# Stick-breaking attention by differences of neighbouring values: the scan's running products are the weights, the mask sits in the scan, and GpSimd adds the halves of the heads

## The chip, the cores and the metric

The kernel runs on one core of a Trainium2 chip. The metric is device time in microseconds of the slowest core, here the only one; a kernel's number is the median of its runs. The engines are TensorE (PE in the profile, its weight loads PEld), VectorE (DVE), ScalarE (ACT), GpSimd (POOL) and SyncE (SP), which issues nearly all DMAs here.

## The reference

One encoder layer on 2048 tokens of width 1024, in float32. A normed and modulated input is projected to queries, keys and values of 16 heads of 64. Eight heads do stick-breaking attention, eight do softmax attention within a band of chunks; the outputs are concatenated, projected, and a squared-ReLU MLP follows. The stick-breaking part, for each query block:

```python
z = jnp.einsum('bqhd,bkhd->bhqk', qb, kb).astype(jnp.float32) * scale
strict = s_idx < t_idx
log_beta = jax.nn.log_sigmoid(z)
log_1m_beta = jnp.where(strict, jax.nn.log_sigmoid(-z), 0.0)
suffix = lax.cumsum(log_1m_beta, axis=3, reverse=True) - log_1m_beta
w = jnp.where(strict, jnp.exp(log_beta + suffix), 0.0)
outs.append(jnp.einsum('bhqk,bkhd->bqhd', w.astype(v.dtype), vb))
```

The weight of a key is its own sigmoid times the product of (1 - sigmoid) over all the keys between it and the query.

## The kernel before

The host hands the sequence over in reverse, so a query attends to later positions and the product over the keys between runs forward. All large products are made of three fp32r matmuls on a high and a low part of each operand (`mm3`); `split` makes the parts with an ACT cast and a subtraction on VectorE or GpSimd. Rows are taken in four blocks of 512 tokens (`TB`), numbered 0 to 3, and blocks of the reversed sequence are worked on from 3 down to 0.

**Projection stage** (to about 421 us). A list of jobs, each one piece of the projection weights for one token block, runs on TensorE. `project` (line 343) does one job in four banks; for the stick-breaking values (piece 4) lines 377 to 391 cast each bank [128 tokens x 512] into high and low parts and store them to the scratch `scr_v`. Three such jobs do blocks 3, 2 and 1; that of block 1, `(1, 4, 1)`, is the last job of all, and runs when the first attention units' operands are already loaded. `behind` and `later` are lists of work put off by a number of ticks, one tick per bank; in this stage ACT, VectorE, GpSimd, TensorE and SyncE are kept in program order.

**Attention** (421 to 1372 us). Units are listed in lines 1043 to 1046: for each query block g from 3 to 0, first the stick-breaking units `SB(h, g, c)` for eight heads h and all key blocks c from g to 3, then the chunked units `CA(h, g)`. A unit has four steps, one for each 128 queries. The loop of line 1115 runs one step after the other; eight steps behind (`LAG`) follow the transposes of the weights and the products with the values. In each step some matmuls of a *filler* (the rest of the projection, then output projections) are dealt out by a credit that depends on the step alone. Scores go into one of four banks (`pz`, tag `z`), which the transposed weights share.

A step of a stick-breaking unit has, in `scores` (line 776), two matmuls into a bank `z` and, in the diagonal unit (c equal to g), a third in bfloat16 that adds -1e30 where a key is not ahead of the query (`identb`, `maskb`). In `soft1` (line 787) ACT makes the sigmoid `b` and then, in place, the sigmoid of the negated scores; VectorE scans that one into running products `p`, started by the last product of the unit before (`carry`); GpSimd puts the start into column 0 of `p` and multiplies `b` by `p` shifted by one. The products `b` are the weights; TensorE transposes them (`transposes`), ACT and VectorE split them (`parts`: `wth`, `wtl`), TensorE multiplies them with the parts of the values (`values`) into `acc`, whose two halves of 64 partitions hold the products with the high and the low part.

At the end of a head `finish` (line 693) adds the halves: ACT copies one into `otmp`, VectorE adds the other into `o`. After two heads `keep` (line 705) splits `o` and stores it for the output projection.

The values of block 0 are projected by the filler during attention (`fill_qkv`, line 926); `keep` in line 963 stores them as parts.

## Time and profile before

| | |
|---|---|
| median of 3 runs | 2667.61 us (2666.88 to 2668.83) |
| profiled execution, first to last instruction (span) | 2672.1 us |
| PE busy, matmuls | 2598.4 us (97%) |
| DVE busy | 1929.1 us (72%) |
| ACT busy | 1511.7 us (57%) |
| POOL busy | 919.8 us (34%) |
| attention | 421 to 1372 us of the span |

Of the profiled execution only the span is known. In the rows, tiles are named without their numbers: `z` is a bank of stick-breaking scores, `cz` one of chunked scores, `wt` one of transposed weights, `pt` one of the projection stage, `pf` and `po` those of the filler, `cols` are small columns of the softmax. All the engines' instructions go through one helper (line 42), so the line tells nothing and the tile does. A matmul's end is modelled, so matmuls overlap in the timeline and the time that one takes is read from start to start.

### The profile page before, as it was taken

What the parts mean: (1) busy time and instruction counts of PE and PEld (TensorE: products, weight loads), DVE (VectorE), ACT (ScalarE), POOL (GpSimd) and SP (SyncE); (2) the same over time, 40 slices, a digit from 0 to 9 for tenths busy, and PEclk for the clock granted to TensorE, in tenths of its full rate; (3) what the DMA queues carried; (4) which work ended last, traced back from release to release, by engine and by line L of the source; (5) the groups of instructions that cost most, each with busy time, mean ns of one, the idle gap of its engine ahead of it and who ended that gap; (6) DMA issues with size and microseconds to landing.
All of it is one profiled execution on the core that took longest, in us unless ns stands there. A gap on an engine that the chain in (4) does not pass through costs nothing. (4 is left out here: it accounts for less than half of the span.)

```text
span 2672.1 us, 40291 instructions
## 1 busy us (share of the span) xinstructions
PE 2598.4 (97%) x12944; PEld 2162.5 (81%) x12944; DVE 1929.1 (72%) x3287; ACT 1511.7 (57%) x2962; POOL 919.8 (34%) x1192
## 2 busy tenths in 40 slices
PE   6999999898999999999999999999999999999999
PEld 5888887687878887778788888878888888888887
DVE  7656766698789878989768787677857656555555
ACT  5333436787688878878654444456544545444443
POOL 4330144576467656767522323100002323200000
PEclk9999999999999999999999999999999999999999
DMA  9879888988887687756677777786675343465574
GB/s 339 307 300 363 313 318 261 262 255 258 251 260 249 203 260 251 236 191 206 208 276 274 273 255 266 252 322 221 222 265 175 138 166 140 148 250 197 194 266 156
DMA packets 263061, 651.28 MB, mean 244 GB/s; under 512 B 29632, under 2 KB 61376, under 8 KB 252992
## 3 DMA queue, kind: packets, MB, share of 16 engines
q1 hardware_dynamic: 261552, 643.98, 70.5%
q10 hardware_dynamic: 1296, 4.72, 0.4%
q8 instruction: 103, 1.69, 0.3%
q14 instruction: 110, 0.90, 0.1%
HBM read 457.21 MB, written 191.37 MB: 243 GB/s over the span
## 5 line engine op out<-in xcount | busy, mean ns | idle before, releaser
L42 PE MATMUL ps<-oph,opv 128*128 128x512 f32 x2688 | 612.5, 390 | 0.3
L42 PE MATMUL ps<-h,opw 128*128 128x512 f32 x2664 | 607.0, 390 | 4.3 <-DVE cx L42 4.3
L42 PEld LDWEIGHTS ps<-oph,opv 128*128 128x128 f32 x2688 | 503.8, 188 | 107.0 <-DVE opv L42 1.2
L42 PEld LDWEIGHTS ps<-h,opw 128*128 128x128 f32 x2664 | 500.6, 188 | 110.3 <-DVE cx L42 5.8
L42 POOL TENSOR_TENSOR b<-b,p 128x512 f32<-128x512 f32 (+1 forms) x320 | 360.3, 1126 | 197.9 <-DVE p L42 176.6
L42 DVE TENSOR_TENSOR wtl<-wt,wth 128x512 fp32r<-128x512 f32 (+3 forms) x544 | 290.5, 545 | 52.5 <-ACT wth L42 50.0
L42 ACT CAST wth<-wt 128x512 fp32r<-128x512 f32 (+3 forms) x544 | 257.8, 485 | 118.8 <-PE wt L42 104.0
L42 DVE TENSOR_TENSOR oph<-hw,oph 128x512 fp32r<-128x512 f32 x224 | 156.4, 698 | 220.4 <-ACT oph L42 220.4
L42 ACT CAST oph<-hw 128x512 fp32r<-128x512 f32 x224 | 139.5, 623 | 283.3 <-PE ps L42 267.2
L42 PE MATMUL pt<-w,ht 128*128 128x512 f32 x1248 | 288.7, 391 | 2.2 <-DVE qh L42 2.2
L42 POOL TENSOR_TENSOR ts<-w 128x512 f32<-128x512 f32 x32 | 44.8, 1400 | 668.4 <-DMA w<-in_w_dram 576.7
L42 PEld LDWEIGHTS pt<-w,ht 128*128 128x128 f32 x1248 | 232.8, 188 | 50.5 <-ACT csq L42 2.9
L42 DVE TENSOR_TENSOR_SCAN p<-z,p,zero 128x512 f32<-128x512 f32 x192 | 246.1, 1282 | 34.6 <-ACT z L42 29.2
L42 PE MATMUL acc<-wth,v 128*128 128x512 f32 (+3 forms) x544 | 222.6, 413 | 0.8 <-ACT wth L42 0.8
L42 ACT ACTIVATE b<-z 128x512 f32<-128x512 f32 (+1 forms) x320 | 171.7, 537 | 65.7 <-PE z L42 48.3
L42 PE MATMUL z<-k,q 128*128 128x512 f32 (+3 forms) x640 | 186.5, 373 | 9.7 <-DVE p L42 7.2
L42 POOL TENSOR_TENSOR e<-e,cols 128x640 f32<-128x640 f32 (+4 forms) x128 | 143.2, 1123 | 146.1 <-DVE cols L42 81.3
L42 PE MATMUL acc<-wtl,v 128*128 128x512 f32 (+3 forms) x544 | 187.1, 350 | 0.0
L42 DVE TENSOR_TENSOR opw<-w,opw 128x512 fp32r<-128x512 f32 x127 | 103.8, 819 | 113.1 <-ACT opw L42 113.0
L42 PE MATMUL wt<-ident,b 128*128 128x128 f32 x1088 | 173.3, 275 | 6.8 <-DVE cols L42 5.1
L42 ACT ACTIVATE z<-z 128x512 f32<-128x512 f32 (+1 forms) x320 | 170.4, 532 | 0.0
L42 PEld LDWEIGHTS wt<-ident,b 128*128 128x128 f32 x1088 | 134.8, 142 | 37.9 <-DVE cols L42 6.7
(193 smaller groups left out, 4257.6 us busy)
## 6 DMA issues: line engine op xcount, KB each, us to landing
hw<-scr_hid SPq DMA_DIRECT2D x112, 512.0 KB, 3.9
k<-scr_k SPq DMA_DIRECT2D x272, 128.0 KB, 4.2
v<-scr_v SPq DMA_DIRECT2D x136, 256.0 KB, 4.3
q<-scr_q SPq DMA_DIRECT2D x128, 256.0 KB, 5.4
w<-in_w_dram SPq DMA_DIRECT2D x64, 512.0 KB, 5.2
hw<-scr_s SPq DMA_DIRECT2D x64, 512.0 KB, 4.6
fw<-scr_w SPq DMA_DIRECT2D x28, 1024.0 KB, 7.0
wa<-in_w_ada_dram SPq DMA_DIRECT2D x48, 512.0 KB, 6.3
```

Of the source, the lines that this page charges most:

```text
L42: return lambda *x, **y: self.tc.keep_in_program_order(f(*x, **y))
```

## The change

Let p(t) be the running product up to and with key t. The weight of key t is p(t-1) - p(t), so the output is the first value plus the sum over t of p(t) times (value of t+1 minus value of t), with a zero behind the last value. The change uses that:

- The scan's products are transposed as they are. The first sigmoid, the seed column and GpSimd's product are gone; `p` now lives in the pool of twelve (`zw`) in which `b` lived, and the pool `zp` has four tiles instead of six.
- Stored as values are differences of neighbouring rows. The raw values go to a new scratch `scr_r` (with a row of zeros behind the last), are read back shifted by one row, GpSimd subtracts, and then the difference is split and stored as before.
- The mask is in the diagonal scan: its second operation is the maximum with a tile `held` that is 1 where the key is not ahead of the query and 0 elsewhere, so the product stays 1 up to the query. The mask matmul is gone. The first value of each query tile is gathered into `vcol` by a DMA of single elements and added to the head's output.
- `finish` copies both halves with ACT into `o` and `otmp`; once for two heads, GpSimd adds them and, in a further operation, `vcol`.

```diff
@@ values of blocks 3 to 1, in project and behind it
+                if kind == 2 and not ca:
+                    step_values(tb, tt, ps, nm)
+                    yield
+                    continue
...
+        def step_values(tb, tt, ps, nm):
+            raw = stp.tile([P, TB], F32, tag="qh", name=f"vr{nm}_{tt}", bufs=6)
+            act.copy(raw, ps)
+            sp.dma_start(raw_rows(tb, tt, 1, slice(None))[:, 0], raw)
+            waiting.append((tt, raw))
+            for n in range(1 if tt < 3 else 2):
+                if waiting[0][0] == tt and tt < 3:
+                    break
+                t, r = waiting.pop(0)
+                behind.add(2 + n, lambda t=t, r=r: follow(tb, t, r, nm))
+            if tt == 3:
+                behind.add(2, lambda: first_values(tb, range(NH // 2)))
...
+        def follow(tb, t, raw, nm):
+            nx = stp.tile([P, TB], F32, tag="qh", name=f"vn{nm}_{t}", bufs=6)
+            sp.dma_start(nx, next_rows(tb, t, 1, slice(None))[:, 0])
+            def less():
+                pool.tensor_tensor(nx, nx, raw, op=ALU.subtract)
+            def parts():
...
+                    split(sv[:, :, t % 2, 0, :], sv[:, :, t % 2, 1, :], half)
...
+            behind.add(1, less)
+            behind.add(2, parts)
@@ finish
-            tmp = op.tile([P, TB], F32, tag="otmp", name=f"otmp{u.nm}")
             act.copy(tmp[r : r + HD, :], u.acc[q : q + HD, :])
-            dve.tensor_tensor(o[r : r + HD, :], u.acc[r : r + HD, :], tmp[r : r + HD, :], op=ALU.add)
+            act.copy(o[r : r + HD, :], u.acc[r : r + HD, :])
             if u.h % 2:
-                soon.append(lambda: keep(u, o))
+                soon.append(lambda: total(u, o, tmp))
+        def total(u, o, tmp):
+            pool.tensor_tensor(o, o, tmp, op=ALU.add)
+            if not u.ca:
+                c = vcol[:, u.h // 2, 4 * u.g : 4 * u.g + 4].unsqueeze(2).to_broadcast([P, 4, P])
+                o4 = o.rearrange("p (t c) -> p t c", c=P)
+                pool.tensor_tensor(o4, o4, c, op=ALU.add)
+            soon.append(lambda: keep(u, o))
@@ scores
-                pe.matmul(z[:, :n], self.q[:, 1, qs], self.k[:, c0:], start=False, stop=not self.diag)
-                if self.diag:
-                    pe.matmul(z[:, :P], identb, maskb, start=False, stop=True)
+                pe.matmul(z[:, :n], self.q[:, 1, qs], self.k[:, c0:], start=False, stop=True)
@@ soft1
-                act.activation(b[:, :n], z[:, :n], AF.Sigmoid, scale=0.125)
                 act.activation(z[:, :n], z[:, :n], AF.Sigmoid, scale=-0.125)
-                before = ones[:, 0:1] if self.diag else self.carry[qi]
-                pool.tensor_copy(pt[:, 0:1], before)
...
-                pool.tensor_tensor(b[:, :n], b[:, :n], pt[:, :n], op=ALU.mult)
+                if self.diag:
+                    dve.tensor_tensor_scan(pt[:, :n], z[:, :n], held[:, :n], 1.0, op0=ALU.mult, op1=ALU.max)
+                else:
+                    dve.tensor_tensor_scan(
+                        pt[:, :n], z[:, :n], zero.to_broadcast([P, n]), self.carry[qi], op0=ALU.mult, op1=ALU.add
+                    )
+                self.carry[qi] = pt[:, n - 1 : n]
+                self.ws.append((pt, c0))
@@ start of attention, behind the last job and the first scores
+        behind.flush()
         later.flush()
```

The values of block 0 go the same way through `late_values` and `late_follow`, with `later` for `behind`, in two copies and two differences for each half of the heads.

The order of the instructions where attention begins, first ACT before. Names: `pt_4_1_3` is the last bank of the last values job, `sv` its parts, `px` and `st` are chunked keys; `z_0_3_3_0` is head 0, query block 3, key block 3, step 0.

```order
L42 CAST sv_4_1_2_1_3887<-pt_4_1_2_3861 128x4x64
L42 ACTIVATE st_8_0_2_3897<-px_8_0_2_3892,gqk_s 128x512
L42 ACTIVATE st_8_0_3_3906<-px_8_0_3_3901,gqk_s 128x512
L42 CAST sv_4_1_2_0_3886<-pt_4_1_3_3910 128x4x64
L42 CAST sv_4_1_2_1_3887<-pt_4_1_3_3910 128x4x64
L42 ACTIVATE b_0_3_3_0_3977<-z_0_3_3_0_3941 128x512
L42 ACTIVATE z_0_3_3_0_3941<-z_0_3_3_0_3941 128x512
```

ACT after, at the same place; `vr` are raw values, `vn` the shifted ones, which by then hold the differences.

```order
L42 ACTIVATE st_8_0_3_3957<-px_8_0_3_3952,gqk_s 128x512
L42 COPY vr_4_1_3_3986<-pt_4_1_3_3961 128x512
L42 CAST sv_4_1_0_0_3995<-vn_4_1_0_3941 128x4x64
L42 CAST sv_4_1_0_1_3996<-vn_4_1_0_3941 128x4x64
L42 CAST sv_4_1_0_0_3995<-vn_4_1_1_3989 128x4x64
L42 CAST sv_4_1_0_1_3996<-vn_4_1_1_3989 128x4x64
L42 CAST sv_4_1_2_0_4017<-vn_4_1_2_4001 128x4x64
L42 CAST sv_4_1_2_1_4018<-vn_4_1_2_4001 128x4x64
L42 CAST sv_4_1_2_0_4017<-vn_4_1_3_4003 128x4x64
L42 CAST sv_4_1_2_1_4018<-vn_4_1_3_4003 128x4x64
L42 ACTIVATE z_0_3_3_0_3992<-z_0_3_3_0_3992 128x512
```

Before, two casts straight from the bank stand between the last bank and the first sigmoid; now a copy and the casts of all four differences do. VectorE's eight subtractions stand ahead of its first scan in the same way.

TensorE at this place, before; `k` and `q` are the operands of the scores.

```order
L42 MATMUL pt_4_1_3_3910<-w_4_7_3728,ht_7_2636 128x512 x3
L42 MATMUL z_0_3_3_0_3941<-k_0_3_3_3768,q_0_3_3765 128x512 x2
L42 LDWEIGHTS identb
L42 MATMUL z_0_3_3_0_3941<-maskb,identb 128x128
L42 MATMUL z_0_3_3_1_3984<-k_0_3_3_3768,q_0_3_3765 128x384 x2
```

TensorE after; `pf` is the filler.

```order
L42 MATMUL pt_4_1_3_3961<-w_4_7_3781,ht_7_2689 128x512 x3
L42 MATMUL z_0_3_3_0_3992<-k_0_3_3_3826,q_0_3_3823 128x512 x2
L42 MATMUL z_0_3_3_1_4065<-k_0_3_3_3826,q_0_3_3823 128x384 x2
L42 MATMUL z_0_3_3_2_4075<-k_0_3_3_3826,q_0_3_3823 128x256 x2
L42 MATMUL z_0_3_3_3_4083<-k_0_3_3_3826,q_0_3_3823 128x128 x2
L42 MATMUL z_1_3_3_0_4089<-k_1_3_3_3832,q_1_3_3829 128x512 x2
L42 MATMUL pf_2_0_4092<-ht_0_2682,fw_2_0_4068 128x512 x3
```

The mask's weight load and matmul are gone from each diagonal step; the first filler matmul stands behind the fifth scores, as before.

More of the change, by code (lines that the diff above doesn't have):

```diff
@@ L115, in encoder_kernel @@
     make_identity(nc, ident)
-    identb = cpool.tile([P, P], BF16, name="identb")
-    dve.tensor_copy(identb, ident)
-    maskb = cpool.tile([P, P], BF16, name="maskb")
-    pool.memset(maskb, 0.0)
-    pool.affine_select(
-        out=maskb, in_=maskb, pattern=[[1, P]], base=0, channel_multiplier=-1,
-        compare_op=ALU.is_gt, fill=NEG,
-    )
+    vcol = cpool.tile([P, 2, NH // 2, 4 * NTB], F32, name="vcol")[:, 0]
+    pool.memset(vcol, 0.0)
     ones = cpool.tile([P, P], F32, name="ones")
@@ L664, in encoder_kernel @@
         sp = nc.sync
+        held = kp0.tile([P, TB], F32, tag="held", name="held", bufs=1)
+        pool.memset(held, 0.0)
+        pool.affine_select(
+            out=held[:, :P], in_=held[:, :P], pattern=[[1, P]], base=0, channel_multiplier=-1,
+            compare_op=ALU.is_gt, fill=1.0,
+        )
         def load_q(ca, h, g):
@@ L972, in fill_qkv, with late_values, late_follow, less @@
                     yield keep
+        raws = {}
+        def late_values(tb, hf, j, ps, nm):
+            cols = slice(hf * CW, (hf + 1) * CW)
+            raw = raws[j] = fp.tile([P, 2, CW], F32, tag="vr", name=f"vr{nm}", bufs=2)
+            act.copy(raw, ps.rearrange("p (t c) -> p t c", t=2))
+            sp.dma_start(raw_rows(tb, 2 * j, 2, cols), raw)
+            if not j:
+                return
+            for i in range(2):
+                later.add(1 + i, lambda i=i, raw=raws[i]: late_follow(tb, hf, i, raw, nm))
+            later.add(2, lambda: first_values(tb, (2 * hf, 2 * hf + 1)))
+        def late_follow(tb, hf, j, raw, nm):
+            nx = xrp.tile([P, 2, CW], F32, tag="xr", name=f"vn{nm}_{j}")
+            sp.dma_start(nx, next_rows(tb, 2 * j, 2, slice(hf * CW, (hf + 1) * CW)))
+            def less():
+                pool.tensor_tensor(nx, nx, raw, op=ALU.subtract)
+            def parts():
+                store_v(0, nx.rearrange("p t c -> p (t c)"), fp, hf, tb, j, f"{nm}_{j}")
+                stepped.add((tb, hf, j))
+            later.add(1, less)
+            later.add(2, parts)
+        stepped = set()
         def outproj(self, g):
```

43 lines of the change are left out of this document (32 added, 11 removed).

## The prediction

> **What bounds the kernel now.** I read the stages first: busy time of each engine in the eight stretches of attention (for the query blocks 3, 2, 1, 0 in turn: stick-breaking units, then chunked units). The columns are the stretch, its length, then PE, weight loads, DVE, ACT and POOL busy, the granted clock and the DMA share.
>
> ```profile
> 421.00:470.00 49.00, 46.39 (x268) 36.17 (x267) 38.33 (x64) 38.27 (x99) 32.66 (x61) 0.97 0.92 275
> 470.00:526.00 56.00, 46.09 (x258) 38.21 (x256) 37.43 (x135) 38.74 (x107) 27.15 (x38) 0.91 0.94 269
> 526.00:649.00 123.00, 118.56 (x758) 102.32 (x757) 106.92 (x150) 101.86 (x220) 84.66 (x136) 0.99 0.79 247
> 649.00:737.00 88.00, 80.13 (x463) 67.93 (x462) 62.34 (x220) 56.95 (x130) 42.79 (x35) 0.94 0.88 264
> 737.00:928.00 191.00, 187.66 (x1193) 161.91 (x1193) 170.98 (x226) 158.19 (x328) 130.01 (x197) 1.00 0.75 235
> 928.00:1009.00 81.00, 78.49 (x517) 69.50 (x515) 64.48 (x223) 57.67 (x133) 43.10 (x36) 1.00 0.89 267
> 1009.00:1272.00 263.00, 256.15 (x1408) 209.69 (x1408) 233.72 (x298) 213.00 (x426) 193.94 (x280) 0.99 0.68 218
> 1272.00:1372.00 100.00, 96.02 (x583) 81.57 (x582) 76.22 (x250) 66.54 (x152) 49.50 (x43) 1.00 0.66 206
> sum 951.00, PE 909.50 PEld 767.31 DVE 790.42 ACT 731.21 POOL 603.82; mean PE 113.69 PEld 95.91 DVE 98.80 ACT 91.40 POOL 75.48
> ```
>
> TensorE is busy 909.5 of 951 us: 41.5 us is all the idle time there is to win. The clock column adds a little: 0.03 x 49 + 0.09 x 56 + 0.01 x 123 + 0.06 x 88 + 0.01 x 263 is about 16 us of lost speed. VectorE is nearly as full in the stick-breaking stretches (233.7 of 263), so it is the second bound. After 1372 us the change touches nothing.
>
> Next, who ended the idle time between 421 and 1372: first TensorE's waits, then VectorE's (us in total, times, longest).
>
> ```profile
> PE wt L42 <- DVE cols L42: 9.3, 6, 2.5
> PE z L42 <- DVE p L42: 7.2, 11, 2.3
> PE cz L42 <- DVE cols L42: 6.2, 9, 1.8
> PE pf L42 <- DMA fw<-scr_w: 5.7, 2, 3.8
> PE cz L42 <- DMA k<-scr_k: 5.6, 3, 2.6
> DVE wtl L42 <- ACT wth L42: 50.0, 93, 7.2
> DVE p L42 <- ACT z L42: 46.1, 95, 2.8
> DVE o L42 <- ACT otmp L42: 28.1, 41, 1.4
> ```
>
> TensorE waits 22.7 us for VectorE and 11.3 us for weights and keys. VectorE in turn waits 46.1 us for the sigmoid ahead of its scan and 28.1 us for the copy ahead of a head's sum. No engine waits long for GpSimd's product.
>
> **The change part by part.** The groups of instructions that it removes (count | busy, mean ns | idle before):
>
> ```profile
> L42 ACT ACTIVATE b<-z 128x512 f32<-128x512 f32 x224 | 134.4, 600 | 50.4 <-PE z L42 37.5 <-POOL p L42 7.0 <-POOL b L42 3.0
> L42 POOL TENSOR_TENSOR b<-b,p 128x512 f32<-128x512 f32 x224 | 289.5, 1292 | 179.5 <-DVE p L42 164.7 <-DVE cols L42 9.9 <-DMA k<-scr_k 0.8
> L42 DVE TENSOR_TENSOR o<-acc,otmp 64x512 f32<-64x512 f32 x64 | 44.0, 687 | 28.5 <-ACT otmp L42 28.1
> L42 PE MATMUL z<-maskb,identb 128*128 128x128 bf16 x128 | 29.6, 231 | 0.0
> ```
>
> *Mask matmuls.* 128 of them go, with their weight loads. The 231 ns overlap their neighbours, so the slot has to be read from the timeline: a full-width step with the mask, then one without.
>
> ```profile
> 1240.20 0.62 PE L42 MATMUL z<-k,q 128*128 128x512 f32 x2
> 1240.67 0.23 PE L42 MATMUL z<-maskb,identb 128*128 128x128 bf16 x1
> ...
> 1247.62 0.63 PE L42 MATMUL z<-k,q 128*128 128x512 f32 x2
> 1248.09 0.62 PE L42 MATMUL po<-fx,ow 128*128 128x512 f32 x2
> ```
>
> From scores to what follows the pair is 0.47 us in both; the filler behind the mask began at 1240.71, so the mask takes 0.04 us. 128 x 0.04 = 5 us gained on TensorE itself; 29.6 us is the upper end.
>
> *The first sigmoid, the product and its seed.* 172 us of ACT and 360 us of GpSimd go, mostly hidden. What shows is the 46.1 us in which the scan waited for ACT: the remaining sigmoid now comes first, one activation (0.6 us) sooner.
>
> *A head's sum.* VectorE loses 64 x 0.687 = 44 us and the 28 us of waits before them. ACT gains 64 copies of about 0.58 us into the 172 us it loses; GpSimd gains 32 + 16 sums of about 1.29 us into the 360 us it loses. Their rows:
>
> ```profile
> L42 ACT COPY otmp<-acc 64x512 f32<-64x512 f32 x64 | 37.2, 582 | 2.8 <-PE acc L42 1.3
> L42 POOL TENSOR_TENSOR os<-o,os 128x512 fp32r<-128x512 f32 x32 | 41.1, 1286 | 17.3 <-ACT os L42 16.3
> ```
>
> The block's output is up to 2.6 us later, hidden by the filler; behind the last unit, some 18 us lie between its store and the first product with the reloaded tiles (1373.6 and 1391.8). Without that cover it would cost 2.6 us once.
>
> ```profile
> L42 ACTq DMA_DIRECT2D scr_m<-os x1: 325/325/325, 1373.6 to 1373.6; - x1
> L42 PE MATMUL pso<-opm,ow x72: 389/389/389, 1391.8 to 1407.9; 128*128 128x512 f32 x72
> ```
>
> *What that relief is worth.* VectorE is relieved of some 118 us of work and waiting, but TensorE can only give back what it loses: 22.7 us behind VectorE and about 16 us of clock. The filler's matmuls are dealt out by step, so where TensorE is full nothing moves. I take half of the waits (11), a fifth of the clock (3) and 5 us for idle time shorter than the modelled end of a matmul: 19 us. From below 5 (all hidden), from above 40 (all of the 22.7, the 16 and a bit).
>
> *Neighbour differences in the projection stage.* Blocks 3 and 2 each get four copies, stores, shifted reloads and GpSimd differences in place of casts straight from the bank. The stretch holding most of them:
>
> ```profile
> 200.00:300.00 100.00, 100.00 (x458) 83.13 (x457) 61.90 (x106) 40.37 (x79) 2.40 (x9) 1.00 1.00 370
> ```
>
> TensorE is full, ACT and GpSimd have room; the DMA engines are full. About 4.2 MB more at 370 GB/s is 11 us of transfer time, hidden because TensorE waits for no load there; with that cover gone, up to 11 us. I take 1. The gathers of first values have no row here: between nothing and a key load's landing each, waited for by GpSimd alone; 0. Block 0's values come late, among the filler: four copies and four differences on engines that have room, no scan behind them; 0.
>
> *The start of attention.* This is the cost. The last values job (block 1) finishes as attention begins, and its parts are flushed there: ACT's and VectorE's queues have its eight casts and eight subtractions ahead of the first sigmoid and scan, and they wait for store, reload and difference. TensorE has only four scores to do; the fifth needs a bank that the first scan frees. Queued behind that wait are the filler on TensorE and every soft step on ACT and VectorE. Before (scores, the last cast; loads and stores with KB and median us to landing; the landing line is that of the value stores; an issue on SyncE; a diagonal scan):
>
> ```profile
> 421.14 0.61 PE L42 MATMUL z<-k,q 128*128 128x512 f32 x2
> 424.88 0.98 PE L42 MATMUL z<-k,q 128*128 128x512 f32 x2 [1.22 <-DVE p L42]
> 421.34 0.37 ACT L42 CAST sv<-pt 128x256 fp32r<-128x256 f32 x1 [3.88 <-PE pt L42]
> v<-scr_v SPq DMA_DIRECT2D x136, 256.0 KB, 4.3
> scr_x<-xr SPq DMA_DIRECT2D x21, 256.0 KB, 3.9
> DMA to landing us min/median/max: 2.9/6.5/8.5
> 427.90 0.58 SPq L687 DMA_DIRECT2D v<-scr_v  x1
> L42 DVE TENSOR_TENSOR_SCAN p<-z,zero 128x512 f32<-128x512 f32 x32 | 39.1, 1222 | 14.7 <-ACT z L42 12.5 <-PE z L42 1.2 <-issue 0.7
> ```
>
> After: copy 421.3 to 421.9; store landed 3.9 later (425.8); SyncE issues two loads of 0.58 ahead (1.2), the reload lands 4.3 later (431.3); difference 1.3, two casts 0.75, sigmoid 0.6, scan 1.2: 435.2. The fifth scores move from 424.9 to 435.2, 10.3 us later. With both transfers at 6.5 us it is 15.1; with 2.9 us each, 8. On SyncE four gathers and four stores of parts stand ahead of the fourth unit's operands, and the stores wait for VectorE; that unit scores twelve steps in, so nobody waits. On GpSimd only the mask tile's setting and the differences themselves are queued.
>
> *The clock there.* Two stretches around the present stall:
>
> ```profile
> 421.80:425.20 3.40, 1.66 (x11) 1.20 (x11) 2.40 (x4) 2.99 (x9) 0.23 (x1) 1.00 0.92 337
> 425.20:428.60 3.40, 3.40 (x10) 2.36 (x9) 2.59 (x4) 1.18 (x3) 3.17 (x6) 0.50 1.10 384
> ```
>
> A stretch in which TensorE was half idle is followed by 3.4 us at half clock, 1.7 us of work lost. That loss exists already, and a longer stall should bring at most one more such stretch: 0 to 1.7, I take 1. The Trainium skill (TensorE: Matmul & The Clock Gate, What's actually happening) says that the clock falls to half after at least one idle window of about 3.4 us and returns after one busy window. The trace agrees on length and ratio, but shows it for 1.74 us of idle in 3.4. By the page's rule the long stall pays one gated window, as now, and the sum would have 0 here.
>
> **The sum.** -5 (mask) - 19 (waits, clock) + 10.3 + 1 (start) + 1 (projection) = -11.7 us on a span of 2672.1: 2660.4. The profiled span lies 4.5 us above the median of the runs, 2667.6; carried over, the forecast is 2656.
>
> **The rivals.** *The start costs more than attention gives back.* Place: 421 to 440 us. Two full-price transfers make the stall 15.1, the clock 1.7 and the projection stage 2; attention returns only the mask's 5 and another 4, because the filler paces it. That is +9.8: 2677.4. It decides once the stall costs more than the waits return. For it: the queues' order makes the chain certain, and DMA is at 0.92 or more there. Against it: 22.7 us of TensorE's waits name VectorE, which gets 12% of the 951 us back. Chance 0.17.
>
> *A wash.* The stall at 10.3 and the gains at 11 cancel: 2667. It holds if half-idle VectorE waits are replaced by waits for the filler's weights. Chance 0.14.
>
> *VectorE was the real bound.* Then nearly all of the 22.7 goes, half of the clock's 16, and short idle time doubles to 10: 5 + 22 + 8 + 10 against 12 is -33: 2635. For it: 89% in the longest stretch, and scan plus subtraction fill a step. Against it: the same stretch has TensorE at 97%. Chance 0.17.
>
> *The change does not do what it says.* The maximum in the 128 diagonal scans could be dearer than the addition. The present ones take 1222 ns for 512 columns, 2.4 ns each; 32 rows of 512 + 384 + 256 + 128 columns make 98 us, and at twice the price as much again would land on a full VectorE: some 80 us slower than the forecast.
>
> Against it: nothing but the operation differs; 0.03, outside the range.
>
> **How the numbers follow.** Forecast 0.49 at 2656, larger gain 0.17, wash 0.14, slower 0.17, dear scan 0.03. The forecast's own bounds (gains of 18 to 34, costs of 10 to 14) run from 2644 to 2664. The range takes in the larger gain and most of the slower case: 2634 to 2675. A measurement tells about 0.2% (5.3 us) from no change, so faster means below 2662.3: the larger gain and most of the forecast and a bit of the wash, 0.66. Same 0.15, slower (above 2672.9) 0.19.
>
> **What would show it.** Right: no mask rows; the scan's wait for ACT well below 46.1 us; TensorE idle some 10 us between 423 and 436 with ACT's casts of the differences just before the first sigmoid; TensorE's waits for VectorE near half. Wrong: the stall under 5 or over 16; attention from the first block's fifth scores to the last sum shortened by less than 10 us or more than 35; diagonal scans above 1.3 us; waits for loads in the projection stage.

## The result

| | before | after |
|---|---|---|
| median, same chip | 2668.22 us (2666.88 to 2669.58, 4 runs) | 2689.03 us (2687.63 to 2689.82, 4 runs) |
| ratio, 95% interval | | 1.0076 (1.0061 to 1.0090) |
| span of the profiled execution | 2672.1 us | 2688.0 us |
| first attention scores | 421.1 us | 442.0 us |
| first scores to the output projection (`pso`) | 970.7 us | 968.4 us |

The change is slower, by 0.8%, where it was forecast to be faster, and lies above the predicted range of 2634 to 2675. By the spans +15.9 us: +20.9 before attention begins, -2.3 in attention, -2.7 behind it. (The span of the profiled execution of before lies 3.9 us above the median in this table; the ratio is the better measure of the whole, the spans of where it lies.) Ratios are taken between runs of the same round and leave out single runs far off the rest, such as one of 9155 us among the six of two_late_sbuf.

### The profile after

The stages of attention, in the order and columns in which the prediction shows them for before:

```profile
442.00:500.00 58.00, 43.12 (x234) 36.24 (x233) 37.97 (x66) 32.37 (x78) 11.14 (x9) 0.85 0.89 262
500.00:556.00 56.00, 46.48 (x259) 37.92 (x259) 32.45 (x130) 43.61 (x118) 32.65 (x39) 0.94 0.98 280
556.00:672.00 116.00, 113.81 (x723) 101.22 (x724) 98.17 (x137) 80.88 (x163) 18.10 (x17) 0.99 0.81 257
672.00:761.00 89.00, 77.56 (x459) 65.44 (x459) 58.53 (x215) 58.91 (x135) 46.08 (x37) 0.96 0.88 263
761.00:962.00 201.00, 189.07 (x1167) 166.71 (x1166) 166.52 (x216) 124.77 (x248) 23.55 (x19) 0.97 0.74 233
962.00:1041.00 79.00, 77.51 (x514) 68.95 (x514) 61.63 (x219) 60.46 (x138) 46.16 (x38) 1.00 0.91 274
1041.00:1293.00 252.00, 247.61 (x1378) 206.70 (x1376) 225.27 (x284) 162.97 (x309) 36.95 (x33) 1.00 0.71 228
1293.00:1391.00 98.00, 95.42 (x587) 81.87 (x586) 70.94 (x241) 70.17 (x160) 55.27 (x48) 1.00 0.68 206
```

Two stick-breaking stretches became shorter (123 to 116, 263 to 252), and two longer: the first (49 to 58) and that of query block 1 (191 to 201), where TensorE now idles 12 us. GpSimd is nearly empty (37 us busy of 252 in the longest stretch, 194 of 263 before). So the work is gone, but time was added in these two places, and in a third, ahead of attention.

TensorE's longest waits in attention, and the scan's wait for the sigmoid (us in total, times, longest):

```profile
PE z L42 <- DVE p L42: 27.5, 9, 14.1
PE pf L42 <- DMA fw<-scr_w: 8.1, 1, 8.1
PE wt L42 <- DVE cols L42: 5.7, 5, 1.8
PE cz L42 <- DMA k<-scr_k: 4.4, 3, 2.5
DVE p L42 <- ACT z L42: 57.8, 107, 3.3
```

Scores wait 27.5 us for a bank that a scan frees, 7.2 before, 14.1 of them in one piece. The scan's own wait for ScalarE, which was to fall well below 46.1 us, rose to 57.8.

Groups that the change altered (the remaining sigmoid, the full-width diagonal scan, the heads' sum, the second copy):

```profile
L42 ACT ACTIVATE z<-z 128x512 f32<-128x512 f32 x224 | 130.7, 584 | 48.5 <-PE z L42 45.3 <-DVE p L42 1.2
L42 DVE TENSOR_TENSOR_SCAN p<-z,held 128x512 f32<-128x512 f32 x32 | 39.0, 1218 | 19.8 <-ACT z L42 19.8
L42 POOL TENSOR_TENSOR o<-o,otmp 128x512 f32<-128x512 f32 x32 | 41.4, 1292 | 285.3 <-ACT o L42 244.0 <-DMA q<-scr_q 27.7 <-DMA k<-scr_k 13.4
L42 ACT COPY o<-acc 64x512 f32<-64x512 f32 x64 | 37.2, 581 | 0.8
```

The scan with the maximum takes 1218 ns, 1222 with the addition: that rival is out.

**Ahead of attention.** Rows picked from the timeline of after, from 285 us: SyncE's issues (SPq), ScalarE and GpSimd around the differences (in brackets, how long the engine sat idle before and what ended that), and TensorE's first product for the last block's norm (`pva`).

```profile
288.68 6.16 SPq L42 DMA_DIRECT2D scr_w<-w  x8
291.88 0.41 ACT L42 CAST sv<-vn 128x256 fp32r<-128x256 f32 x1 [13.52 <-DMA scr_v<-sv]
294.88 0.60 SPq L42 DMA_DIRECT2D vn<-scr_r  x1
301.28 1.29 POOL L42 TENSOR_TENSOR vn<-vn,vr 128x512 f32<-128x512 f32 x1 [13.39 <-DMA vn<-scr_r]
302.60 0.72 ACT L42 CAST sv<-vn 128x256 fp32r<-128x256 f32 x2 [7.76 <-POOL vn L42]
303.22 5.01 ACT L42 ACTIVATE ht<-xt,mod 128x512 fp32r<-128x512 f32 x8
305.31 5.31 SPq L42 DMA_DIRECT2D xt<-in_xT_dram  x8
319.65 1.87 PE L42 MATMUL pva<-ones,nsaa 128*128 128x1 f32 x8 [15.41 <-DVE nsaa L42]
```

The same two steps before the change:

```profile
281.50 5.03 ACT L42 ACTIVATE ht<-xt,mod 128x512 fp32r<-128x512 f32 x8
285.80 6.80 SPq L42 DMA_DIRECT2D xt<-in_xT_dram  x8
```

`ht` is block 1's input, cast from the tiles `xt`; block 0's inputs are loaded into the tiles that it frees. ScalarE, in its order, has the casts of block 2's differences ahead of `ht`. It waits 13.5 us for a staging tile whose store is queued on SyncE, then 7.8 us for a difference whose reload SyncE issued at 294.88, behind eight weight stores. So `ht` comes 21.7 us later, the loads of block 0's inputs 19.5 us later, and TensorE, which had waited for no load here, stands for 15.4 us, until the sums over the late inputs (`nsaa`) are made. Behind that it works until about 326 us at a granted clock of 0.50 (1.00 there before), which costs some 3 us more of the 20.9.

**The start of attention.** The timeline of after, TensorE's fifth scores:

```profile
457.44 1.22 PE L42 MATMUL z<-k,q 128*128 128x512 f32 x2 [14.07 <-DVE p L42]
```

Stretches of 3.4 us around it, in the columns of the stages (length, PE, weight loads, DVE, ACT, POOL, clock, DMA share, GB/s):

```profile
442.00:445.40 3.40, 1.37 (x9) 1.15 (x7) 0.76 (x2) 1.20 (x3) 0.00 (x0) 1.00 1.01 282
445.40:448.80 3.40, 0.00 (x0) 0.00 (x0) 0.00 (x0) 0.00 (x0) 0.00 (x0) 0.53 0.96 333
...
455.60:459.00 3.40, 1.55 (x4) 1.27 (x5) 3.40 (x6) 1.65 (x6) 0.00 (x0) 0.50 0.81 287
459.00:462.40 3.40, 3.40 (x10) 2.82 (x9) 1.36 (x2) 0.35 (x2) 0.00 (x0) 0.50 1.00 285
462.40:465.80 3.40, 3.40 (x20) 2.86 (x20) 2.14 (x4) 1.62 (x5) 0.00 (x0) 0.96 0.21 62
```

The stall is the predicted one, 14.1 us long, with no engine busy at all in the second stretch. From the first to the fifth scores it is 15.4 us (442.0 to 457.4), 3.7 before. The clock returns only after one full stretch of work, 459.0 to 462.4. (The Trainium skill, TensorE: Matmul & The Clock Gate, What's actually happening, says that one busy window of about 3.4 us restores it; this trace agrees.)

**Block 0's late values.** The timeline of after, TensorE's scores in block 1's stretch:

```profile
893.83 1.22 PE L42 MATMUL z<-k,q 128*128 128x512 f32 x2 [6.11 <-DVE p L42]
```

The waits from 885 to 896 us:

```profile
ACT svf L42 <- POOL vnf L42: 7.2, 1, 7.2
DVE svf L42 <- ACT svf L42: 7.0, 1, 7.0
PE z L42 <- DVE p L42: 6.1, 1, 6.1
POOL vnf L42 <- DMA vnf<-scr_r: 5.3, 1, 5.3
```

The casts of `vnf`, the late differences, come two ticks behind their reload; every sigmoid and scan behind them waits too. A second such stall, of 3.7 us, follows near 930 us. In this stretch TensorE idles some 10 us more than in the kernel without the differences (below), and is busy 5 to 6 us longer at a clock of 0.97 where that one has 1.00; these make up the 15 us by which the stretch is longer.

### The profile page after: what moved, and what is told of

Its sections match the earlier page's. It is cut to its first block, busy times and chain, and to the rows that moved or that the text cites. A ratio compares the mean times of both kernels' runs of the same rounds, so it can differ in the third digit from the quotient of the medians.

```text
span 2688.0 us, 38753 instructions
## 1 busy us (share of the span) xinstructions
PE 2583.0 (96%) x12816; PEld 2163.1 (80%) x12816; DVE 1884.6 (70%) x3222; ACT 1417.6 (53%) x2722; POOL 604.2 (22%) x617
## 5 line engine op out<-in xcount | busy, mean ns | idle before, releaser
L42 PE MATMUL z<-k,q 128*128 128x512 f32 (+3 forms) x640 | 186.8, 374 | 29.9 <-DVE p L42 27.5
L42 PE MATMUL wt<-ident,p 128*128 128x128 f32 x1088 | 172.2, 274 | 4.4 <-DVE cols L42 2.9
L42 PEld LDWEIGHTS wt<-ident,p 128*128 128x128 f32 x1088 | 134.8, 141 | 35.3 <-DVE cols L42 5.7
L42 PE MATMUL po<-fx,ow 128*128 128x512 f32 x576 | 160.3, 393 | 0.0
L42 PEld LDWEIGHTS z<-k,q 128*128 128x128 f32 x640 | 115.1, 191 | 52.5 <-DVE p L42 31.5
```

The source lines that it names most:

```text
L42: return lambda *x, **y: self.tc.keep_in_program_order(f(*x, **y))
```

## The experiments

The theory after reading the traces is called Q in the expectations: attention gives back about what was forecast, and making the differences costs some 40 us in three places, because ScalarE and VectorE stand, in order, behind casts that wait for a reload. Rival B says that it is not the order but the bytes, which stand on full DMA engines and on SyncE's queue ahead of the loads that matter. Kernels named plain, idle or free, and the one without gathers, leave a part of the computation out, as said for each; all others compute the whole layer.

### The change without its differences: plain_values

This kernel casts the value parts straight from the banks, and leaves out the raw copies, their stores and reloads, the differences and the first values.

```diff
-                if kind == 2 and not ca:
-                    step_values(tb, tt, ps, nm)
...
-                            late_values(tb, hf, j, ps, nm)
+                            store_v(0, ps, fp, hf, tb, j, nm)
...
```

> The changed kernel, but the value tiles are cast straight from their PSUM banks as before: no raw copy, store, shifted reload, difference or gather (the differences and the first values are left out of the computation; the scan, the mask and the heads' sums stay as changed). Theory Q (the attention stage gives back about what the prediction took, and the making of the differences costs about 40 us by itself: 20.9 in the projection stage, 9.2 at the start of attention, 9.5 where block 0's values come late): 2689 - 40 = 2649, first attention scores at 419 to 424 us. Rival W (attention gives back little, the filler paces it, and the cost of the differences is mostly the shift that they put on everything behind): 2665 or more.

2639.43 us (2638.44 to 2641.98), 0.9902 of before (0.9886 to 0.9917). The stretch from first scores to `pso`, before and here:

```profile
421.10:1391.80 970.70, 929.20 (x5521) 783.59 (x5521) 798.22 (x1572) 736.49 (x1597) 605.11 (x823) 0.98 0.77 241
```

```profile
421.50:1359.70 938.20, 902.36 (x5394) 774.72 (x5393) 753.82 (x1506) 635.00 (x1340) 262.42 (x232) 0.99 0.80 248
```

The scan, mask and sums alone gain 32.5 us in the profiled executions, and 26 us (22 to 30) by the ratio; theory Q expected too small a gain (2649), rival W is out. Its first five stretches:

```profile
421.50:464.80 43.30, 40.75 (x234) 34.26 (x233) 35.05 (x60) 29.60 (x71) 7.24 (x6) 1.00 1.01 294
464.80:520.40 55.60, 46.51 (x260) 37.75 (x258) 32.67 (x131) 43.85 (x118) 32.67 (x39) 0.94 1.00 285
520.40:636.20 115.80, 113.77 (x723) 101.15 (x723) 97.90 (x137) 80.72 (x163) 17.99 (x17) 0.99 0.82 255
636.20:725.80 89.60, 78.17 (x465) 66.02 (x464) 59.16 (x216) 59.29 (x136) 46.07 (x37) 0.96 0.88 267
725.80:911.20 185.40, 183.11 (x1162) 161.90 (x1161) 164.53 (x216) 122.63 (x242) 18.52 (x15) 1.00 0.76 241
```

Against this kernel the whole change loses 20.5 us before attention, 14.5 at its start (57.8 against 43.3 us to the first chunked scores) and 15.1 in block 1's stick-breaking stretch (200.5 against 185.4): together 50.1, of 51.3 us between the spans.

### The traffic with nobody waiting: idle_reload, free_reload

idle_reload keeps copies, stores, reloads and gathers, but casts the parts from the banks and leaves the differences out:

```diff
                     step_values(tb, tt, ps, nm)
-                    yield
-                    continue
...
-            behind.add(1, less)
-            behind.add(2, parts)
...
```

> As plain_values, but the raw copies, their stores, the shifted reloads and the gathers are all issued where the changed kernel issues them; only nothing waits for what they bring (the parts are cast from the banks; the differences are left out). Theory Q (the cost is ScalarE waiting in its order behind parts that wait for the reload and for the landing of the value store): within 4 us of plain_values, 2649 to 2653, first scores before 426 us. Rival B (the cost is the traffic and the issue time on SyncE, 4.2 MB more in a stage whose DMA engines are full): 15 us or more above plain_values, first scores at 435 or later.

2665.37 us (2662.33 to 2676.65), ratio 0.9991 (0.9976 to 1.0006); first scores at 436.2. Q's bound, within 4 us of plain_values, is missed (26 us above it); B's is met. Its `ht` casts and its loads:

```profile
282.29 5.02 ACT L42 ACTIVATE ht<-xt,mod 128x512 fp32r<-128x512 f32 x8
...
300.41 6.42 SPq L42 DMA_DIRECT2D xt<-in_xT_dram  x8
```

`ht` is on time, and still block 0's loads are issued 14.6 us later than before: SyncE gets to them late. That is about the worth of 4.2 MB at 370 GB/s, 11.3 us by estimate, and of the gathers, 3.9 us by the run without them (below). The start of attention loses to the traffic alone as well: 52.8 us to the first chunked scores, against 43.3 in plain_values and 57.8 in the change, with 1.4 us of waits for a scan in all, but one of 5.0 us for a load. In block 1's stretch, though, nothing is lost (185.8 us): there it is the waiting, not the traffic.

free_reload is idle_reload with reloads that read the same number of bytes from the input; it asks whether SyncE was late because it waits, in order, for each raw store to land:

```diff
-            sp.dma_start(nx, next_rows(tb, t, 1, slice(None))[:, 0])
+            sp.dma_start(nx, xT[t * P : (t + 1) * P, tb * TB : (tb + 1) * TB])
```

> As idle_reload (which had its first attention scores at 436.2 and 2665 us, against 421.5 and 2639 without the traffic), but the shifted reloads of blocks 3, 2 and 1 read as many bytes, in the same rows of 2 KB, from the input, so that they wait for no store to land (differences left out). Theory B (bytes: 4.2 MB at the 370 GB/s of that stage are 11 us, the gathers 4): no change, first scores 434 to 437, 2661 to 2668. Rival O (SyncE waits in its order for each raw store to land, and all later loads stand behind): first scores at 428 or earlier, 2655 or less.

2665.59 us, ratio 0.9988 (0.9979 to 0.9998), first scores at 435.1. No change: rival O is out.

### Another queue, and no gathers: reload_gp, no_gathers

reload_gp is the whole change with the shifted reloads of blocks 3 to 1 issued by GpSimd:

```diff
-            sp.dma_start(nx, next_rows(tb, t, 1, slice(None))[:, 0])
+            pool.dma_start(nx, next_rows(tb, t, 1, slice(None))[:, 0])
```

> The changed kernel, whole, with one edit: the shifted reloads of blocks 3, 2 and 1 are issued by GpSimd, on its own DMA queue, not by SyncE behind the bulk stores of weights. Theory Q (the reload comes late because it stands behind those stores on SyncE's queue): most of the 20.9 us of the projection stage returns, first scores at 424 to 432, 2689 - 10 to 18 = 2671 to 2679. Rival B (traffic): no change, 2685 to 2692. Rival G (the gathers): no change either. A third possibility: GpSimd, waiting in its own order for the store to land, delays the norms' reciprocal roots, and the gain is halved.

2693.35 us, ratio 1.0106 (1.0089 to 1.0123), first scores at 443.1. Q's number is missed, and the time is next to B's 2685 to 2692: `ht` comes 4 us sooner than in the change (299.2) and the loads still later (307.2). The reloads land no faster from there (median 5.1 us on either queue).

no_gathers leaves the first values at zero:

```diff
-                behind.add(2, lambda: first_values(tb, range(NH // 2)))
...
-            later.add(2, lambda: first_values(tb, (2 * hf, 2 * hf + 1)))
```

> The changed kernel without the twelve gathers of first values (the first values stay zero: that part of the sum is left out). Theory Q: they hold SyncE for 3.4 us ahead of the store that ScalarE waits for, so 3 to 8 us come back in the projection stage, and 2 to 4 where block 0's values come late: 2678 to 2684. Rival G (the 4-byte transfers are what is dear: they crowd the DMA engines): the whole 20 us come back, 2665 to 2670. If they are hidden, as the prediction took: 2686 to 2691.

2686.26 us, ratio 1.0078 (1.0060 to 1.0096); first scores at 438.1, 3.9 us sooner than in the change. The time lies at the edge of what was expected if they are hidden (2686 to 2691), and by the ratio nothing can be told; by the trace of one execution the gathers, taken at 0, are worth 3.9 us ahead of attention. G is out.

### Two terms of the gain: plain_oldsum, plain_maskmm

Both are plain_values with one thing of before put back.

```diff
-            act.copy(o[r : r + HD, :], u.acc[r : r + HD, :])
+            dve.tensor_tensor(o[r : r + HD, :], u.acc[r : r + HD, :], tmp[r : r + HD, :], op=ALU.add)
```

> As plain_values (2639 us), but a head's two halves are added by VectorE from the bank as before the change (64 adds of 0.69 us), and GpSimd adds only the first values. Theory V (VectorE's share is what the attention stage gives back): 8 to 15 us slower than plain_values, 2647 to 2654, the attention stage (first scores to the output projection, 938.2 us in plain_values) 946 to 953. Rival F (the shorter feed of the scan, one sigmoid in place of two, gave it back; the sum was hidden): 0 to 3 us slower.

2643.02 us (2642.48 to 2644.36): 3.6 slower than plain_values, in the profile 943.9 against 938.2 us of attention. Between the two theories: 64 sums of 0.69 us and their waits were worth a tenth to a fifth of what attention gave back.

```diff
-                pe.matmul(z[:, :n], self.q[:, 1, qs], self.k[:, c0:], start=False, stop=True)
+                pe.matmul(z[:, :n], self.q[:, 1, qs], self.k[:, c0:], start=False, stop=not self.diag)
+                if self.diag:
+                    pe.matmul(z[:, :P], identb, maskb, start=False, stop=True)
```

> As plain_values (2639 us), but the 128 mask matmuls of before are put back behind the scores of the diagonal tiles (the scan keeps its mask tile; the result of the scan is the same). The prediction's term: 128 x 0.04 = 5 us slower, 2644. Upper end of the prediction: 29.6 us of busy time, 2669. If TensorE has slack there: 2639 to 2641.

2644.55 us, 5.1 slower, in the profile 6.6 (944.8). The prediction's 128 x 0.04 = 5 us is met; the upper end, 29.6, is far off. The intervals of these two ratios (0.9891 to 0.9920 and 0.9902 to 0.9937) overlap with that of plain_values, so the times alone don't show either cost; the medians and the stretches agree in sign.

### The waits moved: late_wide, start_later, both_late

late_wide puts the steps of block 0's late values further apart, and its gathers four ticks later:

```diff
-                later.add(1 + i, lambda i=i, raw=raws[i]: late_follow(tb, hf, i, raw, nm))
+                later.add(4 + i, lambda i=i, raw=raws[i]: late_follow(tb, hf, i, raw, nm))
...
-            later.add(1, less)
-            later.add(2, parts)
+            later.add(3, less)
+            later.add(5, parts)
```

> The changed kernel, whole, with only the steps between block 0's late values moved: reload 4 and 5 steps after the store (was 1 and 2), difference 3 steps behind the reload (was 1), parts 5 (was 2). Theory Q (ScalarE and VectorE, in order, stand behind parts that wait for store, reload and difference): most of the 15 us that the stretch of stick-breaking for block 1 has over plain_values comes back, 2689 - 11 to 15 = 2674 to 2678, and no stall of TensorE near 888 and 930 us. Rival B (the traffic there): no change, 2685 to 2690.

2680.81 us, ratio 1.0043 (1.0028 to 1.0058), against 1.0076 for the change. Block 1's stretch falls from 200.5 to 186.7 us and the two stalls are gone, as Q said; 8 us of the time, not 11 to 15.

start_later takes block 1's differences out of the start of attention; they come from step 8 on, with the raw rows reloaded too, and with the casts five steps behind the reload:

```diff
+            if tb == 1:
+                return
             waiting.append((tt, raw))
...
+            later.add(8 + 6 * n, lambda hf=hf, j=j: late_follow(1, hf, j, None, f"e1_{hf}"))
```

> The changed kernel, whole, with one thing moved: block 1's values, whose job ends as attention begins, are only copied and stored there; their reload (raw and shifted rows), difference, casts and parts come from step 8 of attention on, in four portions. Theory Q (the stall at the start is the chain store, reload, difference, casts ahead of the first sigmoid): the stretch from the first scores to the first chunked scores falls from 57.8 to 43 to 46 (43.3 with no differences at all), 2689 - 12 to 15 = 2674 to 2677. Rival B (what is late at the start is the backlog of transfers; with nothing waiting for the reload the stretch still took 52.9): 52 to 54, 2684.

2683.80 us, ratio 1.0047 (1.0029 to 1.0065). The stretch falls from 57.8 to 48.9 us: between the two theories. As this edit takes away both the waiting and the transfers at that place, it can't tell the two apart; idle_reload (52.8 us) says that the transfers had a large part. The stall is gone; but TensorE still waits 6.6 us for scans ahead of scores and 3.9 us ahead of chunked ones, where block 1's portions now stand.

both_late has the two edits together.

> start_later and late_wide together, whole. Theory Q, additive: 2689 - 8 - 13 = 2667 to 2669, level with before; the projection stage keeps its 20 us. Rival B: 2675 to 2677.

2670.45 us, ratio 1.0000 (0.9986 to 1.0014). By the stretches the two add up: 49.9 us at the start, 185.3 in block 1's. Of the 28.9 us by which its span still exceeds that of plain_values, 20.3 lie ahead of attention, in the projection stage, and 6.6 at the start.

### Fewer bytes: sbuf_shift, sbuf_112, sbuf_after

sbuf_shift is both_late with blocks 3 and 2 shifted from one SBUF tile to the next, not by way of DRAM, and with all gathers of first values in attention:

```diff
-            sp.dma_start(nx, next_rows(tb, t, 1, slice(None))[:, 0])
+            sp.dma_start(nx[0 : P - 1, :], raw[1:P, :])
+            sp.dma_start(nx[P - 1 : P, :], scr_r[r : r + 1, :] if up is None else up[0:1, :])
```

> both_late, whole, and blocks 3 and 2 are shifted by one row without the way through DRAM: one transfer from rows 1 to 127 of the raw tile to rows 0 to 126 of the next one, and one of a single row; only each tile's first row is stored, and the gathers of first values come in the first steps of attention. Theory B (bytes ahead of the next block's inputs set the delay): 2.1 MB in place of 4.2 and no gathers, 6 us in place of 15 to 20: first scores at 426 to 429, both_late minus 13 to 16. Rival Q2 (ScalarE's wait for the reload, not the bytes): the chain is one transfer shorter, first scores at 430 to 436. If a transfer within SBUF is dearer than one to DRAM and back: no change.

2737.15 us, ratio 1.0238 (1.0219 to 1.0257): half the bytes, and 67 us slower than both_late. Neither B nor Q2 expected that. From 240 to 280 us, and within it two stretches in which hardly anything but the shifts is moved:

```profile
240.00:280.00 40.00, 21.18 (x97) 17.40 (x95) 3.91 (x9) 4.89 (x11) 5.57 (x8) 0.77 0.32 117
...
248.00:250.00 2.00, 2.00 (x11) 1.65 (x10) 0.00 (x0) 0.00 (x0) 0.00 (x0) 1.00 0.07 26
250.00:252.00 2.00, 2.00 (x11) 1.65 (x10) 0.00 (x0) 0.00 (x0) 0.00 (x0) 1.00 0.07 26
```

The DMA engines are busy 0.32 of the time, moving 117 GB/s, and during the shifts 0.07, moving 26 GB/s: that is about one engine in 16 (0.06). SyncE's issues of `vn<-vr` take up to 9.3 us each. sbuf_after, with block 2's shifts put further back, only moves this:

> As sbuf_shift, whole, and block 2's shifts are put six jobs later, behind the loads of the last block's inputs. Theory B: half of the remaining bytes leave the path too, first scores at 421 to 425, 3 to 5 us below sbuf_shift, 2646 to 2652, against 2639 for no differences at all. Rival: ScalarE's casts, now later, delay the next block's normalization instead, and nothing or less is gained.

2729.95 us, ratio 1.0198 (1.0175 to 1.0220). sbuf_112 is sbuf_shift with the 127 rows cut in two:

```diff
-            sp.dma_start(nx[0 : P - 1, :], raw[1:P, :])
+            for lo, hi in ((0, 112), (112, P - 1)):
+                sp.dma_start(nx[lo:hi, :], raw[lo + 1 : hi + 1, :])
```

> sbuf_shift (2737 us) with one edit: the transfer of 127 rows is issued as one of 112 and one of 15 rows. Theory E (127 rows are dealt to one of the 16 DMA engines, 127 x 84 ns = 10.7 us, while 112 are dealt out evenly): first scores at 426 to 435, 2655 to 2665. Rival S (a transfer from one SBUF tile to another is slow by itself, or the small transfers are): 2720 or more, first scores at 490 or later.

2668.60 us, ratio 1.0000 (0.9990 to 1.0009). One edit returns the 67 us; the same window:

```profile
240.00:280.00 40.00, 40.00 (x186) 33.34 (x185) 24.59 (x43) 13.28 (x31) 10.54 (x13) 1.00 0.83 285
```

So theory E holds in its mechanism: the transfer of 127 rows was not spread over the DMA engines. (The Trainium skill, DMA: Bandwidth & Descriptors, Why a DMA increments its semaphore by 16 and not by 1, says that the number of engines is the largest up to 16 that divides the row count, so that 127 rows use one; the share of 0.07 agrees.) But its number is missed: first scores at 437.8, only the gathers' 4 us better than both_late. Halving the bytes by itself bought nothing:

```profile
298.21 5.02 ACT L42 ACTIVATE ht<-xt,mod 128x512 fp32r<-128x512 f32 x8
300.40 7.51 SPq L42 DMA_DIRECT2D xt<-in_xT_dram  x8
```

Here the loads follow `ht` at once, and `ht` is late behind the casts. There are two chains, the loads' place on SyncE's queue and `ht` behind the casts, and the later one decides:

| kernel | `ht` cast from | `xt` loads from | first scores |
|---|---|---|---|
| before | 281.5 | 285.8 | 421.1 |
| plain_values | 281.8 | 286.5 | 421.5 |
| idle_reload (traffic, no order) | 282.3 | 300.4 | 436.2 |
| free_reload | 280.3 | 298.6 | 435.1 |
| no_gathers | 299.4 | 301.5 | 438.1 |
| sbuf_112 (order, less traffic) | 298.2 | 300.4 | 437.8 |
| the change | 303.2 | 305.3 | 442.0 |
| two_late (below) | 283.0 | 293.0 | 429.5 |
| two_late_sbuf (below) | 280.3 | 288.9 | 426.8 |

First scores come 135 to 138 us behind the loads in every row. Traffic alone puts the loads at 298 to 300, the order of the casts, with half the traffic, at 300: that is why a remedy for one of them by itself showed little.

### Both chains: two_late, two_late_sbuf

two_late is both_late with only copies and stores of block 2 left in the projection stage; its differences are made in attention:

```diff
-            if tb == 1:
+            if tb < 3:
                 return
...
+        for tb, n0 in ((2, 30), (1, 80)):
+            for n, (hf, j) in enumerate(product(range(2), range(2))):
+                later.add(n0 + 6 * n, lambda tb=tb, hf=hf, j=j: late_follow(tb, hf, j, None, f"e{tb}_{hf}"))
...
-            later.add(3, less)
-            later.add(5, parts)
+            later.add(6 if tb else 3, less)
+            later.add(8 if tb else 5, parts)
```

> both_late, whole, and block 2's values are made late as well: in the projection stage they are only copied and stored (1 MB in place of 1 MB of stores, 1 MB of reloads and 2 MB of parts), reload, difference and parts come from step 30 of attention on, block 1's from step 80, each difference 6 and its casts 8 steps behind the reload (3 and 5 in both_late); the gathers of blocks 3, 2 and 1 come in attention. Theory B (bytes that stand on SyncE's queue ahead of the last block's inputs decide): fewer bytes stand there than before the change, so first scores at 420 to 426, and 2642 to 2652, faster than before by 0.6 to 1.0%. Rival P (block 3's chain, ScalarE in order behind the reload, decides): first scores at 430 or later, 2655 or more.

2659.25 us (2656.48 to 2660.93), ratio 0.9964 (0.9950 to 0.9977): faster than both kernels, though not by the 0.6 to 1.0% expected. Its two steps:

```profile
283.04 5.03 ACT L42 ACTIVATE ht<-xt,mod 128x512 fp32r<-128x512 f32 x8
...
293.01 7.44 SPq L42 DMA_DIRECT2D xt<-in_xT_dram  x8
```

The time is in P's range (2655 or more), but not by P's mechanism: `ht` is on time. The loads are 7 us late, where B had them on time. Block 3's raw store and reload and block 2's raw store, in place of block 2's parts, make a megabyte more than before in the stage, ahead of them; whether its bytes or SyncE's waits are the 7 us was not tried apart. 12 us more go where block 2's portions now stand, in the stretch of chunked units (67.7 against 55.6 us in plain_values).

two_late_sbuf shifts block 3 within SBUF (112, 15 and 1 rows) and starts block 2's portions at step 8, eight apart.

> two_late (2659 us, first scores at 429.5, 20 us above the kernel with no differences), whole, with the two remainders attacked: block 3 is shifted within SBUF (rows in 112, 15 and 1), so that 1 MB and one transfer of its chain leave the projection stage; and block 2's late portions come from step 8, eight steps apart, not from step 30, six apart, where a weight load of the filler waited 9.8 us. If both remainders are what two_late's trace names: first scores at 424 to 427, the stretch from there to block 2's first scores at 100 to 104 (110.4 in two_late), 2647 to 2653. If the portions cost the same wherever they stand in a stage whose DMA engines are full: 2655 to 2660.

2658.38 us, ratio 0.9954 (0.9938 to 0.9969). First scores come at 426.8, and 104.3 us lie from there to block 2's first scores, about as the first theory said; but the time is in the range of the second, 2655 to 2660, by which the portions cost the same wherever they stand. The later stretches lose some of it again (block 2's own, with block 1's portions in it, is 118.5 us against 114.9). Between the times of this kernel and two_late nothing can be told.

## Why the prediction was wrong

*Neighbour differences in the projection stage, +1: the step that failed most.* It called 11 us of transfer time "hidden because TensorE waits for no load there". TensorE waited for none because block 0's loads came just in time; the quoted stretch ended at 300 us, and the wait came at 304; the last sums over these inputs were done some 2 us before TensorE came to them (299.9 and 301.9). The bound "with that cover gone, up to 11" was the size of one of the two chains (idle_reload: 14.7 with the gathers); the other, ScalarE's order behind the reloads, was not looked for in this stage at all, though the prediction saw the same chain at the start of attention. Measured: 20.5 us.

*Block 0's late values, 0: failed.* "Engines that have room, no scan behind them": the scans are on the same queue. A cast that waits for a reload holds up every sigmoid behind it, however empty the engine is. Measured: 15.1 us in that stretch; late_wide, which moves only the distances, takes 13.8 of it away.

*The gathers, 0: too small.* 3.9 us ahead of attention, by one execution each; they are part of the 20.5.

*The start of attention, +10.3 and +1: right mechanism, and near in size.* In the prediction's own measure, first to fifth scores, it is 11.7 us (15.4 against 3.7). The stretch as a whole lost 14.5 us against plain_values. The store's 3.9 us was a median over the whole kernel; here the raw store took 5.7 and the reloads 4.0 (medians from 442 to 458 us, the DMA queue 91% busy). On the clock, TensorE worked 5.2 us at half speed behind the stall (457.4 to 462.7), 3.4 before: 0.9 us more lost, by estimate, as forecast. What the prediction left out is the traffic: the transfers alone, with nobody waiting for them, cost 9.5 us there (idle_reload). So the stall and the traffic overlap, and how the 14.5 us divide between them was not tried apart.

*The mask, -5: right* (5.1 by the time, 6.6 by the stretch).

*The waits and the clock, -19: right in size.* Mask and the rest were to give 24; plain_values gave 26 (22 to 30) by the ratio, 32.5 between the profiled executions. The parts were off. TensorE's waits for VectorE, 22.7 before, are in plain_values:

```profile
PE wt L42 <- DVE cols L42: 5.7, 5, 1.8
PE z L42 <- DVE p L42: 4.6, 7, 1.9
PE cz L42 <- DVE cols L42: 3.5, 5, 0.9
```

13.8, so 8.9 us went, near the forecast half. The clock, forecast at 3 of 16, gave half: its stretches below full speed there cost 0.06 x 55.6 + 0.01 x 115.8 + 0.04 x 89.6 = 8.1 us, counted as the prediction counted them. That the scan would wait less for the sigmoid is wrong (57.8 after, 46.1 before). Which of the removed sigmoid, product and seed returned the rest was not tried.

*The rivals.* "The start costs more than attention gives back" had the right sign, but its condition did not hold: the start lost 14.5 us and attention gave back 26 to 32. It had one place of three. Its price, 2677, counted 15.1 and 1.7 us for the start, near the 14.5, and 2 for the projection stage, where 20.5 came; the 15.1 of block 0's values it did not have, and its 9 us for what attention returns were a third of what came. VectorE as the real bound asked for 45 us of gains, and 26 to 32 came. The maximum costs nothing (1218 ns against 1222).

*The signs.* The stall (14.1 us, inside 5 to 16), the diagonal scans and the time from the fifth scores to `pso` (14.0 us shorter, inside 10 to 35) came out as the prediction wanted. The signs against it that appeared are the wait for loads in the projection stage and the scan's wait for ScalarE.

What stays open: the 20 us between the best whole kernels (2658 to 2659) and plain_values. The differences have to be made somewhere, and two_late and two_late_sbuf show some of their cost moving with them; how much could be hidden with the portions spread further was not tried.

## What to carry to other kernels

A transfer between two steps of an in-order engine makes all that is queued behind the second step wait, so such a step belongs as many ticks behind its reload as the reload takes on full DMA engines, whether or not the engine has room. "Nobody waits for a load here" must be read with the margin of the next load on the same queue: block 0's inputs had some 2 us, and all that came behind them was late by about as much as their loads were. When a remedy shows nothing, ask for a second chain of the same length before dropping the theory.

## What the runs showed of the hardware

- While a transfer of 127 rows of 2 KB from one SBUF tile to another ran, the DMA engines' share was 0.07 (26 GB/s), about one engine of 16. Eight of them cost the kernel 67 us: from 240 to 280 us the share was 0.32 (117 GB/s), and 0.83 (285 GB/s) with 112 and 15 rows.
- The shifted reloads landed no faster from another queue: median 5.1 us whether SyncE or GpSimd issued them.
- The clock stayed at half for 17.1 us around a stall of 14.1 us (445.6 to 462.7, from the shares 0.53 and 0.96 of the stretches), and came back after one full stretch of 3.4 us of work.
- A scan of 512 columns took 1218 ns with multiply and maximum, 1222 ns with multiply and addition.
